# Hybrid decoder block on one core: banks copied whole by ScalarE before VectorE subtracts, gate sums started from zeros and bias, two late loads given a place

## The chip, the cores and the metric

The kernel runs on one core of one Trainium2 chip. The metric is the device time of one execution in microseconds (us), as the median of the runs; lower is better. Engines are named as in the profile: PE (TensorE, matmuls; PEld its weight loads), DVE (VectorE), ACT (ScalarE), POOL (GpSimd) and SP (SyncE, which here only issues loads). Each runs its own queue in order.

## The reference

One layer over 256 tokens of width 2048, in float32. All weights are read once, some 190 MB in all. Cut to what matters:

```python
ada = c @ w_ada + b_ada                          # 2048 -> 3 x 2048
shift, scale, gate = jnp.split(ada, 3, axis=-1)
h = rms_norm(x, g_pre) * (1.0 + scale) + shift
proj = h @ w_in                                  # q, k, v of two mixers, their gates, ma, mb
oa = nsa_attention(...)                          # compressed, selected and sliding-window keys
ya = (oa * silu(za)) @ w_br_a
ob = dilated_mixture(...)                        # three dilated windows
yb = (ob * silu(zb)) @ w_br_b
merged = sigmoid(ma) * ya + sigmoid(mb) * yb
out = merged @ w_out
return x + gate * rms_norm(out, g_post)
```

## The kernel before

Every large product is made from high and low parts. A float32 value is rounded to a PE format (fp32r) as its high part H, and the rest of it is the low part L; a product is H·H + H·L + L·H, three matmuls into one PSUM bank. Wherever a value becomes an operand there is thus a pair of steps: ACT copies it with rounding (H), DVE subtracts that copy from the source (L).

**Weights.** SP loads them in 512 KB pieces into seven buffers `raw`; `prep` (line 479) has ACT make `wH` (line 488) and DVE `wL` (line 489), three buffers of each; `product` (from line 536) issues the matmuls, which write banks of tag `mm` (four of the eight PSUM banks). The list `items` sets the order of the weights; between two items a step of the generator `side_main` (line 701) puts in a piece of everything else. A scheduler then sets the order of each engine's queue by its own estimate of when things are ready, so an edit moves neighbours too. It lets ACT and DVE read one PSUM tile only one after the other, in program order. `behind(i)` (line 212) makes an instruction follow instruction `i` on its own engine.

**Turns.** A tile that has to be transposed goes through PE into the bank of tag `pt`, of which there is one; the next user of that bank waits until the last reader is done. `turn_q` (line 822) turns two blocks of 128 queries: the bank's halves of 64 partitions (b = 0, 1) are copied by ACT into their own half of `AR` (line 832, H), and DVE writes the rest into the other half (line 833, L). `turn_k` (line 835) does the same for keys with two copies and two subtracts for each half (lines 844 to 847). `transA` (line 918) turns the probabilities P through a bank `pt_ps` (copy PH at line 925, subtract PL at 926); the scores `sA` (line 885) need AR. In the compressed branch the keys KC are copied by ACT and DVE (lines 747 and 748).

**The m stage.** When a quarter of 512 columns of the merged branches (MA) is complete, it is turned in two banks `m_ps` (one for 128 tokens each, line 1113; eight banks in all) into the operand of the last product. The target is split by the contraction tiles into groups of unequal length, since the high part lies in buffers freed by the low parts of h. For each group ACT makes mH (line 1119) and DVE mL (line 1120) in turn.

**The gate** is the last third of `ada`, summed on DVE: for each of 32 items of kind "gate" a 128x1024 piece of w_ada times one value of c per partition is added to `gacc` (two halves of 1024 columns, 16 items each). The first item of a half writes gacc with a TENSOR_SCALAR (line 507), the others add with SCALAR_TENSOR_TENSOR (line 509). A matmul with ones sums the partitions later; before it POOL adds the bias `bg` to row 0 (line 1140). The loads `gp` (g_post on all partitions, 1 MB), `bg` and `xr` (x again, 2 MB) are issued by ACT's queue (lines 1130 to 1135), as soon as the scheduler finds their buffers free.

## Time and profile before

| | us |
|---|---|
| median of 3 runs (lowest, highest) | 822.84 (822.63, 825.23) |
| the profiled execution | 823.05 |
| its span, first to last instruction | 821.3 |
| PE busy in it | 793.1 |
| DVE busy | 687.9 |
| ACT busy | 417.7 |
| POOL busy | 92.4 |

The span is what the trace shows; 1.75 us of the profiled execution lie outside it. PE is busy in 97% of the span at a granted clock of the upper level (2.4 GHz), so the places where PE pauses count, and the table of stretches, the list of waits and the timeline show where these are. A row of the timeline gives start and duration of an operation and, in brackets, how long its engine had been idle before it and what released it. The names are the program's: `m_ps` is a PSUM tile, `mL<-m_ps,mH` writes mL from the two others.

### The profile page before, as it was taken

The numbers are of one execution on the slowest core, as the hardware profiler recorded it, in microseconds if no ns is written. First come the engines' busy times: TensorE is split into PE (matmuls) and PEld (weight loads), VectorE is DVE, ScalarE is ACT, GpSimd is POOL, SyncE is SP. The second block draws the span as 40 slices with busy tenths as digits, with TensorE's granted clock in tenths as the row PEclk, the third lists the DMA queues.
The fourth block names the chain that finished last, engine by engine and source line by source line (L and its number), as shares of the span: only waits on it lengthen the run. The fifth ranks groups of instructions, "written<-read, shape, count | busy, mean of one in ns | idle before, by whom it ended". The sixth has DMA issues, their size and how long they took to land.

```text
span 821.3 us, 11929 instructions
## 1 busy us (share of the span) xinstructions
PE 793.1 (97%) x4160; PEld 667.3 (81%) x4160; DVE 687.9 (84%) x1068; ACT 417.7 (51%) x684; POOL 92.4 (11%) x111
## 2 busy tenths in 40 slices
PE   5999999999999999999999999999999999999995
PEld 4487888889887888888789999888887878888884
DVE  4799999999998879899888998867577999967455
ACT  2764263433434646566667666555644344445441
POOL 4200000000000026045412111001000010100000
PEclk9999999999999999999999999999999999999998
DMA  9899899999798547744444435655479999976533
GB/s 328 264 362 313 262 327 309 348 301 339 256 332 310 180 154 255 239 147 136 133 133 138 119 114 177 183 153 154 128 255 325 367 300 343 335 269 231 188 100 103
DMA packets 106950, 193.26 MB, mean 235 GB/s; under 512 B 7593, under 2 KB 36617, under 8 KB 106249
## 3 DMA queue, kind: packets, MB, share of 16 engines
q1 hardware_dynamic: 105376, 189.17, 69.5%
q10 hardware_dynamic: 1514, 3.33, 1.1%
q8 instruction: 33, 0.54, 0.3%
q14 instruction: 27, 0.22, 0.1%
HBM read 190.38 MB, written 2.10 MB: 234 GB/s over the span
## 4 chain that ended last, share of the span: by engine, by line
PE 85%; DVE 9%; issue 2%; DMA 2%; ACT 1%; DVEq 0%; ACTq 0%; SPq 0%
PE mm L558 21%; PE mm L561 21%; PE mm L559 21%; DVE wL L489 3%; PE mm L553 3%; PE mm L550 3%; PE mm L548 3%; PE mm L540 2%; DVE ST L509 2%; PE pt_ps L921 1%; PE sA L885 1%; PE ada_ps L183 1%; DMA xs<-in_x_dram 1%; DMA raw<-in_w_in_dram 1%; PE pvb_ps L1056 1%
## 5 line engine op out<-in xcount | busy, mean ns | idle before, releaser
L488 ACT ACTIVATE wH<-raw 128x1024 fp32r<-128x1024 f32 (+2 forms) x268 | 267.3, 1000 | 293.0 <-PE mm L559 182.3
L489 DVE TENSOR_TENSOR wL<-raw,wH 128x1024 fp32r<-128x1024 f32 (+2 forms) x268 | 316.4, 1185 | 74.1 <-ACT wH L488 69.2
L558 PE MATMUL mm<-wH,xH 128*128 128x512 f32 (+2 forms) x616 | 237.1, 387 | 1.3 <-DVE KB L631 1.1
L559 PE MATMUL mm<-wH,xL 128*128 128x512 f32 (+2 forms) x616 | 234.3, 382 | 0.0
L561 PE MATMUL mm<-wL,xH 128*128 128x512 f32 (+2 forms) x616 | 188.4, 383 | 0.4 <-DVE wL L489 0.4
L558 PEld LDWEIGHTS mm<-wH,xH 128*128 128x128 f32 x616 | 115.8, 188 | 23.0 <-issue 2.7
L559 PEld LDWEIGHTS mm<-wH,xL 128*128 128x128 f32 x616 | 115.9, 188 | 20.4 <-DVE xL L245 0.3
L561 PEld LDWEIGHTS mm<-wL,xH 128*128 128x128 f32 x616 | 113.1, 188 | 23.2 <-DVE wL L489 1.9
L509 DVE SCALAR_TENSOR_TENSOR ST<-raw,vecT,ST 128x768 f32<-128x768 f32 (+2 forms) x75 | 76.0, 1013 | 3.3 <-DMA raw<-in_w_ada_dram 3.1
L548 PE MATMUL mm<-xH,wH 128*128 128x256 f32 x240 | 63.5, 284 | 1.0 <-DVE VB L631 1.0
L550 PE MATMUL mm<-xL,wH 128*128 128x256 f32 x240 | 63.1, 283 | 0.0
L553 PE MATMUL mm<-xH,wL 128*128 128x256 f32 x240 | 50.0, 284 | 0.4 <-DVE wL L489 0.4
L558 PE MATMUL mm<-wH,yH 128*128 128x512 f32 x128 | 50.2, 392 | 0.0
L559 PE MATMUL mm<-wH,yL 128*128 128x512 f32 x128 | 50.0, 390 | 0.0
L558 PE MATMUL mm<-wH,mH 128*128 128x512 f32 x128 | 49.9, 390 | 0.0
L559 PE MATMUL mm<-wH,mL 128*128 128x512 f32 x128 | 49.9, 390 | 0.0
L548 PEld LDWEIGHTS mm<-xH,wH 128*128 128x128 f32 x240 | 45.9, 191 | 1.6 <-issue 1.6
L509 DVE SCALAR_TENSOR_TENSOR gacc<-raw,vecT,gacc 128x1024 f32<-128x1024 f32 x30 | 38.4, 1278 | 9.3 <-DMA raw<-in_w_ada_dram 9.3
L550 PEld LDWEIGHTS mm<-xL,wH 128*128 128x128 f32 x240 | 45.9, 191 | 0.0
L561 PE MATMUL mm<-wL,mH 128*128 128x512 f32 x128 | 39.8, 389 | 0.0
L561 PE MATMUL mm<-wL,yH 128*128 128x512 f32 x128 | 39.5, 390 | 0.0
L553 PEld LDWEIGHTS mm<-xH,wL 128*128 128x128 f32 x240 | 37.9, 192 | 0.8 <-DVE wL L489 0.8
(296 smaller groups left out, 1003.8 us busy)
## 6 DMA issues: line engine op xcount, KB each, us to landing
raw<-in_w_in_dram SPq DMA_DIRECT2D x165, 512.0 KB, 4.4
raw<-in_w_ada_dram SPq DMA_DIRECT2D x48, 512.0 KB, 5.5
raw<-in_w_ada_dram SPq DMA_DIRECT2D x48, 384.0 KB, 4.7
raw<-in_w_out_dram SPq DMA_DIRECT2D x32, 512.0 KB, 4.8
raw<-in_w_br_a_dram SPq DMA_DIRECT2D x16, 512.0 KB, 5.7
raw<-in_w_br_b_dram SPq DMA_DIRECT2D x16, 512.0 KB, 6.1
raw<-in_w_in_dram SPq DMA_DIRECT2D x29, 256.0 KB, 3.1
raw<-in_w_ada_dram SPq DMA_DIRECT2D x24, 256.0 KB, 4.9
```

Source lines behind the costliest of these rows:

```text
L183: T.matmul(ada0[:, half, j, :], lhsT=raws0[q][:, kk, half, j * 128:(j + 1) * 128], rhs=cT[:, kt:kt + 1].to_broadcast([128, 128]), start=(k ...
L488: A.activation(H, raw, AF.Copy)
L489: V.tensor_tensor(L, raw, H.bitcast(F32), op=OP.subtract)
L509: V.scalar_tensor_tensor(acc, r, cc, acc, op0=OP.mult, op1=OP.add)
L540: T.matmul(job.ps[t][:, :job.n], lhsT=hj[:, t * 128:(t + 1) * 128], rhs=it.raw[:, j, cs], start=(first and j == 0), stop=(last and j == it ...
L548: T.matmul(ps, lhsT=it.H[:, j, bs], rhs=sH[:, it.kt0 + j, :], start=(first and j == 0 and b == 0), stop=False, skip_group_check=True)
L550: T.matmul(ps, lhsT=it.H[:, j, bs], rhs=sL[:, it.kt0 + j, :], start=False, stop=False, skip_group_check=True)
L553: T.matmul(ps, lhsT=it.L[:, j, bs], rhs=sH[:, it.kt0 + j, :], start=False, stop=(last and j == it.nk - 1), skip_group_check=True)
L558: T.matmul(ps, lhsT=sH[:, it.kt0 + j, ts], rhs=it.H[:, j, cs], start=(first and j == 0), stop=False)
L559: T.matmul(ps, lhsT=sL[:, it.kt0 + j, ts], rhs=it.H[:, j, cs], start=False, stop=False)
L561: T.matmul(ps, lhsT=sH[:, it.kt0 + j, ts], rhs=it.L[:, j, cs], start=False, stop=(last and j == it.nk - 1))
L885: T.matmul(o, lhsT=QT[:, u.t, h // 2, h % 2, :], rhs=KTt[:, hl, :, 0:128] if u.t == 0 else KTt[:, hl, u.br, :], start=(hl == 0), stop=(hl ...
```

## The change

1. In the KC loop, in `turn_q`, in `turn_k` and in the m stage all ACT copies of a bank are issued first, and then all DVE subtracts. In the m stage one ACT copy of 128x512 writes a whole mH, and the low part is now what is split into groups.
2. `gacc` is made while attention still runs: POOL zeroes 128x1024 for each half, ACT's queue loads the bias (4 KB) into row 0, and all 32 items add with SCALAR_TENSOR_TENSOR. POOL's adds and the tile `bg` are gone.
3. The load of gp follows the last copy of the second block of the m stage, the reload of x the last copy of the fourth.

```diff
             acc = accs[it.piece][:, :, :it.n // 2]
         else:
-            if it.half not in gacc:
-                need("A")
-                gacc[it.half] = big.tile([128, 1024], F32, name=f"gacc{it.half}", tag=("cv", "k2")[it.half])
+            need("gacc")
             acc = gacc[it.half]
...
-                if it.kt0 + j == 0:
+                if it.kt0 + j == 0 and it.kind == "ada":
                     V.tensor_scalar(acc, r, cc, None, op0=OP.mult)
...
                     src = ps[64 * b:64 * (b + 1), a].rearrange("p t s -> p (t s)")
                     A.activation(KC[0:64, b, :], src, AF.Copy)
+                for b in range(2):
+                    src = ps[64 * b:64 * (b + 1), a].rearrange("p t s -> p (t s)")
                     V.tensor_copy(KC[64:128, b, 0:255], src[:, 1:])
...
                 A.activation(QT[own, t, :, b, :], ps[own], AF.Copy)
+            for b in range(2):
+                own, other = slice(64 * b, 64 * (b + 1)), slice(64 * (1 - b), 64 * (2 - b))
                 V.tensor_tensor(QT[other, t, :, b, :], ps[own], QT[own, t, :, b, :].bitcast(F32), op=OP.subtract)
...
                 A.activation(KTt[own, 0, b, :], psf[own], AF.Copy)
                 A.activation(KTt[other, 0, b, :], psf[own], AF.Copy)
+            for b in range(2):
+                own, other = slice(64 * b, 64 * (b + 1)), slice(64 * (1 - b), 64 * (2 - b))
                 V.tensor_tensor(KTt[own, 1, b, :], psf[own], KTt[own, 0, b, :].bitcast(F32), op=OP.subtract)
                 V.tensor_tensor(KTt[other, 1, b, :], psf[own], KTt[own, 0, b, :].bitcast(F32), op=OP.subtract)
...
+        for half in range(2):
+            gacc[half] = big.tile([128, 1024], F32, name=f"gacc{half}", tag=("cv", "k2")[half])
+            G.memset(gacc[half], 0.0)
+            A.dma_start(gacc[half][0:1, :], b_ada[0:1, 2 * D + half * 1024:2 * D + (half + 1) * 1024])
+        done.add("gacc")
...
-        mH, mL = Parts(), big.tile([128, KT, S], F32R, name="mL", tag="xH")
+        mH, mL = big.tile([128, KT, S], F32R, name="mH", tag="xH"), Parts()
         for a, b in groups:
-            mH.put(lows(a, b, "mH", F32R), a, b)
+            mL.put(lows(a, b, "mL", F32R), a, b)
+        turned = []
...
                 ts = slice(t * 128, (t + 1) * 128)
+                dH = mH[:, 4 * p:4 * p + 4, ts]
+                last = A.activation(dH, ps, AF.Copy, scale=0.5)
                 for a, b in groups:
                     a, b = max(a, 4 * p), min(b, 4 * p + 4)
                     if a < b:
-                        dH, o = mH.at[a]
-                        A.activation(dH[:, a - o:b - o, ts], ps[:, a - 4 * p:b - 4 * p], AF.Copy, scale=0.5)
-                        V.scalar_tensor_tensor(mL[:, a:b, ts], ps[:, a - 4 * p:b - 4 * p], 0.5,
-                                               dH[:, a - o:b - o, ts].bitcast(F32), op0=OP.mult, op1=OP.subtract)
+                        dL, o = mL.at[a]
+                        V.scalar_tensor_tensor(dL[:, a - o:b - o, ts], ps[:, a - 4 * p:b - 4 * p], 0.5,
+                                               dH[:, a - 4 * p:b - 4 * p].bitcast(F32), op0=OP.mult, op1=OP.subtract)
                 if t == NT - 1:
                     done.add(("mT", p))
+                    turned.append(last)
...
-        A.dma_start(gp, bass.AP(tensor=g_post.tensor, offset=g_post.offset, ap=[[0, 128], [1, D]]))
-        bg = big.tile([1, D], F32, name="bg", tag="qb")
-        A.dma_start(bg, b_ada[0:1, 2 * D:3 * D])
-        for t in range(NT):
-            A.dma_start(fin["x"][:, t, :], x[0, t * 128:(t + 1) * 128, :])
+        with behind(turned[1]):
+            A.dma_start(gp, bass.AP(tensor=g_post.tensor, offset=g_post.offset, ap=[[0, 128], [1, D]]))
+        with behind(turned[3]):
+            for t in range(NT):
+                A.dma_start(fin["x"][:, t, :], x[0, t * 128:(t + 1) * 128, :])
...
-            G.tensor_tensor(ga[0:1, :], ga[0:1, :], bg[:, half * 1024:(half + 1) * 1024], op=OP.add)
```

The lists below are pieces of the engines' queues. A row is line, operation, target and sources, shape, and the engines or load queues that it waits for; line numbers after the change are those of the new file.

In the m stage, DVE's queue at the first bank of the first quarter, before:

```order
L489 TENSOR_TENSOR wL<-raw,wH 128x1024 [waits DMAHW7_49,PE_49,Activation_49]
L1120 SCALAR_TENSOR_TENSOR mL<-m_ps,mH_6644 128x128 [waits Activation_49]
L509 SCALAR_TENSOR_TENSOR gacc_6339<-raw,vecT,gacc_6339 128x1024 [waits DMAHW0_49,DVE_49]
L1120 SCALAR_TENSOR_TENSOR mL<-m_ps,mH_6645 128x2x128 [waits Activation_49]
L507 TENSOR_SCALAR gacc_6780<-raw,vecT 128x1024 [waits DMAHW3_49]
L1120 SCALAR_TENSOR_TENSOR mL<-m_ps,mH_6646 128x128 [waits Activation_49]
L642 SCALAR_TENSOR_TENSOR MA<-MA,mm 128x512 [waits PE_49]
L489 TENSOR_TENSOR wL<-raw,wH 128x1024 [waits DMAHW1_49]
L1120 SCALAR_TENSOR_TENSOR mL<-m_ps,mH_6644 128x128 [waits Activation_49]
```

and after the change (the three groups' low parts are three tiles, so their numbers differ):

```order
L489 TENSOR_TENSOR wL<-raw,wH 128x1024 [waits DMAHW7_49,PE_49,Activation_49]
L1132 SCALAR_TENSOR_TENSOR mL_6649<-m_ps,mH 128x128 [waits Activation_49]
L1132 SCALAR_TENSOR_TENSOR mL_6650<-m_ps,mH 128x2x128
L1132 SCALAR_TENSOR_TENSOR mL_6651<-m_ps,mH 128x128
L507 SCALAR_TENSOR_TENSOR gacc_5632<-raw,vecT,gacc_5632 128x1024 [waits DMAHW3_49]
L489 TENSOR_TENSOR wL<-raw,wH 128x1024 [waits DMAHW1_49,PE_49,Activation_49]
L1132 SCALAR_TENSOR_TENSOR mL_6649<-m_ps,mH 128x128 [waits Activation_49]
L1132 SCALAR_TENSOR_TENSOR mL_6650<-m_ps,mH 128x2x128
L1132 SCALAR_TENSOR_TENSOR mL_6651<-m_ps,mH 128x128
```

The gacc rows that stood between the subtracts of one bank now stand behind them, and the TENSOR_SCALAR is a SCALAR_TENSOR_TENSOR.

PE's queue ahead of the second bank of that quarter, before; ahead of these rows stand the first bank and the twelve matmuls of one weight item:

```order
L558 MATMUL mm<-wH,yH_6244 128x512 [waits Activation_49]
L559 MATMUL mm<-wH,yL_6245 128x512
L558 MATMUL mm<-wH,yH_6244 128x512
L559 MATMUL mm<-wH,yL_6245 128x512
L561 MATMUL mm<-wL,yH_6244 128x512 [waits DVE_49]
L561 MATMUL mm<-wL,yH_6244 128x512
L558 MATMUL mm<-wH,yH_6244 128x512
L559 MATMUL mm<-wH,yL_6245 128x512
L1113 MATMUL m_ps<-ident,MA 128x128 [waits DVE_49,PE_49]
L1113 MATMUL m_ps<-ident,MA 128x128 x3
```

and after the change, where the first bank and six matmuls of the same item stand ahead of these rows:

```order
L556 MATMUL mm<-wH,yH_6250 128x512
L557 MATMUL mm<-wH,yL_6251 128x512
L556 MATMUL mm<-wH,yH_6250 128x512
L557 MATMUL mm<-wH,yL_6251 128x512
L559 MATMUL mm<-wL,yH_6250 128x512 x2
L1124 MATMUL m_ps<-ident,MA 128x128 [waits DVE_49,Activation_49]
L1124 MATMUL m_ps<-ident,MA 128x128 x3
L556 MATMUL mm<-wH,yH_6250 128x512
L557 MATMUL mm<-wH,yL_6251 128x512
```

The second bank's transposes moved up by one weight item: twelve matmuls of 128x512 stand between the two banks, where there were twenty.

In attention, ACT's queue at the third `turn_k` (the one at 410 us in the trace of before), before:

```order
L488 ACTIVATE wH<-raw 128x1024 [waits DMAHW1_49,PE_49,Activation_49]
L844 ACTIVATE AR<-k_ps 64x256 [waits PE_49]
L845 ACTIVATE AR<-k_ps 64x256
L488 ACTIVATE wH<-raw 128x1024 [waits DMAHW2_49,PE_49,Activation_49]
L844 ACTIVATE AR<-k_ps 64x256 [waits DVE_49]
L845 ACTIVATE AR<-k_ps 64x256
L488 ACTIVATE wH<-raw 128x1024 [waits DMAHW3_49,PE_49,Activation_49]
```

and after the change:

```order
L488 ACTIVATE wH<-raw 128x1024 [waits DMAHW1_49,PE_49,Activation_49]
L846 ACTIVATE AR<-k_ps 64x256 [waits PE_49]
L847 ACTIVATE AR<-k_ps 64x256
L846 ACTIVATE AR<-k_ps 64x256
L847 ACTIVATE AR<-k_ps 64x256
L488 ACTIVATE wH<-raw 128x1024 [waits DMAHW2_49,PE_49,Activation_49]
```

The four copies of one bank stand together, and the weight copy that stood between them follows.

PE's queue behind the same turn, ahead of the next user of the bank, before (ahead of these rows stand twelve matmuls of 128x512, four sA and three of the four ot_ps rows):

```order
L558 MATMUL mm<-wH,xH 128x512
L559 MATMUL mm<-wH,xL_2455 128x512
L561 MATMUL mm<-wL,xH 128x512
L558 MATMUL mm<-wH,xH 128x512
L559 MATMUL mm<-wH,xL_2455 128x512
L561 MATMUL mm<-wL,xH 128x512
L558 MATMUL mm<-wH,xH 128x512 [waits Activation_49]
L559 MATMUL mm<-wH,xL_1570 128x512
L558 MATMUL mm<-wH,xH 128x512
L559 MATMUL mm<-wH,xL_1570 128x512
L921 MATMUL pt_ps<-ident,P 128x128 [waits DVE_49,PE_49,Pool_49]
L921 MATMUL pt_ps<-ident,P 128x128 x3
```

and after the change (ahead of these rows the same twelve matmuls):

```order
L889 MATMUL sA<-AR 128x256 [waits Activation_49]
L889 MATMUL sA<-AR 128x256 x3
L947 MATMUL ot_ps<-PH,VR 128x256 [waits DVE_49,PE_49,Activation_49]
L925 MATMUL pt_ps<-ident,P 128x128 [waits DVE_49,PE_49,Pool_49]
L925 MATMUL pt_ps<-ident,P 128x128 x3
L949 MATMUL ot_ps<-PL,VR 64x256
L947 MATMUL ot_ps<-PH,VR 128x256
L949 MATMUL ot_ps<-PL,VR 64x256
```

The transposes into pt_ps moved up past three rows of ot_ps and ten matmuls of 128x512.

## Rows read from the trace of the kernel before

**Rows 1.** Busy time of each engine, share of the span, instructions (the page's first part).

```profile
PE 793.1 (97%) x4160; PEld 667.3 (81%) x4160; DVE 687.9 (84%) x1068; ACT 417.7 (51%) x684; POOL 92.4 (11%) x111
```

**Rows 2.** Stretches: limits, length, busy time of PE, PEld, DVE, ACT, POOL, clock, DMA.

```profile
350.00:500.00 150.00, 147.86 (x981) 132.38 (x981) 136.43 (x266) 101.73 (x259) 44.90 (x56) 1.00 0.44 130
600.00:650.00 50.00, 49.61 (x220) 40.75 (x218) 40.71 (x40) 22.01 (x24) 0.00 (x0) 1.00 0.89 319
650.00:700.00 50.00, 48.39 (x221) 39.71 (x220) 49.13 (x56) 20.91 (x27) 2.37 (x1) 1.00 0.95 332
```

**Rows 3.** PE's waits from 300 to 740 us: for whom; total, times, longest (us).

```profile
PE m_ps L1113 <- DVE mL L1120: 1.6, 1, 1.6
PE pt_ps L921 <- DVE AR L833: 0.7, 2, 0.5
PE pt_ps L921 <- DVE AR L847: 0.7, 1, 0.7
PE q_ps L829 <- DVE PL L926: 0.6, 2, 0.3
```

**Rows 4.** Timeline of the m stage's first quarter: start, duration, engine, line, operation.

```profile
657.03 0.60 PE L1113 MATMUL m_ps<-ident,MA 128*128 128x128 f32 x4
...
657.74 0.26 ACT L1119 ACTIVATE mH<-m_ps 128x128 fp32r<-128x128 f32 x1
657.86 1.23 DVE L489 TENSOR_TENSOR wL<-raw,wH 128x1024 fp32r<-128x1024 f32 x1
...
659.21 1.27 DVE L509 SCALAR_TENSOR_TENSOR gacc<-raw,vecT,gacc 128x1024 f32<-128x1024 f32 x1
...
660.40 0.41 DVE L1120 SCALAR_TENSOR_TENSOR mL<-m_ps,mH 128x256 fp32r<-128x256 f32 x1
...
660.56 2.37 POOL L1140 TENSOR_TENSOR gacc<-gacc,bg 1x1024 f32<-1x1024 f32 x1 [79.65 <-DVE gacc L509]
...
660.73 2.75 DVE L507 TENSOR_SCALAR gacc<-raw,vecT 128x1024 f32<-128x1024 f32 x1
...
661.60 0.39 PE L558 MATMUL mm<-wH,yH 128*128 128x512 f32 x1
...
661.83 0.39 PE L559 MATMUL mm<-wH,yL 128*128 128x512 f32 x1
663.40 0.28 DVE L1120 SCALAR_TENSOR_TENSOR mL<-m_ps,mH 128x128 fp32r<-128x128 f32 x1
...
663.83 0.63 PE L1113 MATMUL m_ps<-ident,MA 128*128 128x128 f32 x4 [1.61 <-DVE mL L1120]
```

**Rows 5.** Timeline around the load of gp, from DVE, ACT's queue and PE.

```profile
602.37 0.75 DVE L507 TENSOR_SCALAR gacc<-raw,vecT 128x1024 f32<-128x1024 f32 x1
...
606.28 0.36 ACTq L1130 DMA_DIRECT2D gp<-in_g_post_dram  x1
...
614.52 1.28 DVE L509 SCALAR_TENSOR_TENSOR gacc<-raw,vecT,gacc 128x1024 f32<-128x1024 f32 x1 [4.52 <-DMA raw<-in_w_ada_dram]
...
617.00 0.50 PE L561 MATMUL mm<-wL,xH 128*128 128x512 f32 x1 [0.39 <-DVE wL L489]
```

**Rows 6.** Groups from 340 to 500 us: total and mean (ns); idle before.

```profile
L925 ACT ACTIVATE PH<-pt_ps 128x512 fp32r<-128x512 f32 x23 | 13.7, 597 | 7.6 <-PE pt_ps L921 7.2
```

**Rows 7.** The group of POOL's largest memsets.

```profile
L750 POOL MEMSET BL<- 128x32 f32 x4 | 0.6, 156 | 254.2 <-DVE BL L754 242.6 <-DVE mf L301 11.7
```

**Rows 8.** Timeline of the third key turn.

```profile
410.48 0.38 PE L840 MATMUL k_ps<-ident,K 128*128 128x128 f32 x2
...
411.45 0.37 ACT L844 ACTIVATE AR<-k_ps 64x256 fp32r<-64x256 f32 x1
411.59 1.77 DVE L489 TENSOR_TENSOR wL<-raw,wH 128x1024 fp32r<-128x1024 f32 x1 [0.52 <-ACT wH L488]
...
416.88 0.52 PE L921 MATMUL pt_ps<-ident,P 128*128 128x128 f32 x3
```

**Rows 9.** DVE's longest wait from 676 to 720 us: total, times, longest (us).

```profile
DVE wL L489 <- ACT wH L488: 0.8, 1, 0.8
```

## The prediction

> **What bounds the kernel now.** I read the busy shares first [rows 1]: TensorE (PE) is busy 793.1 of 821.3 us, so what a change can win is the time in which PE stands still. The next view is the table of stretches [rows 2]: from 350 to 500 us PE is busy 147.86 of 150 us, from 600 to 650 us 49.61 of 50, from 650 to 700 us 48.39 of 50. These are the three stretches in which most of the edited code runs, and they lack 2.1, 0.4 and 1.6 us. VectorE (DVE) is busy 49.13 of 50 us in the last one: there a wait of PE is a place in DVE's queue, not a long operation. Third, the list of PE's waits says whom it waits for [rows 3]: once for 1.6 us for the m stage's low part, 0.7 + 0.7 + 0.6 us for the bank tagged pt behind attention's turns and PL. That list counts a little less than starts show: before the next m_ps the last matmul starts at 661.83, one follows another by 0.23 us (661.60 to 661.83), so the next could start at 662.06, and starts at 663.83 [rows 4]: 1.77 us. Measured so, the pauses of over 0.15 us between 340 and 490 us number ten, from 0.16 to 0.84 us, and make 3.9 us. The edited steps thus have some 1.8 + 0.4 + 3.9 = 6.1 us to give.
>
> **The m stage: -1.8 us.** One m_ps bank is copied and subtracted in three groups, in turn by ACT and DVE, because the two engines' reads of one bank stand one after the other. Each of DVE's three subtracts is queued behind something longer [rows 4]: behind wL (657.86, 1.23 us), behind a gacc (659.21), and the last behind the second gate half's first TENSOR_SCALAR, which takes 2.75 us (660.73) while a POOL add of 2.37 us runs (660.56); the same form takes 0.75 us at 602.37 with POOL idle [rows 5]. So the last subtract starts at 663.40, 5.8 us after the transposes' end (657.03 + 0.60). Changed: one ACT copy of 128x512, for which PH, the same shape from the same kind of bank, gives 0.60 us [rows 6]; then three subtracts side by side, 0.28 + 0.41 + 0.28 = 0.97 us [rows 4]. By the order they stand behind the same wL, which ends at 657.86 + 1.23 = 659.09, when the copy (657.74 + 0.60 = 658.34) is done: the last ends at 660.06, and with 0.15 us for the hand-over (663.40 + 0.28 to 663.83) the bank is free at 660.2. PE gets to the second m_ps earlier, since the scheduler counts on the shorter chain: only 12 matmuls stand between, 12 x 0.23 = 2.8 us from 657.6, so 660.4. It arrives as the bank has just come free, and the pause of 1.77 us goes. What is late next: nothing in the list, since the other three blocks have no listed wait now and shed the same exchanges. Bounds: all of it (-1.8), or, if one item like wL (1.23 us) still comes between, -0.6. I take -1.8, as the order shows none.
>
> **Gate sums.** SCALAR_TENSOR_TENSOR takes the place of TENSOR_SCALAR: 1.27 us [rows 4] for 2.75 once (POOL's add is gone from there) and for 0.75 once [rows 5]: on DVE a gain of 1.0 us. It ends on no path of its own; DVE feeds PE through wL. The two zeroings of 128x1024 on POOL have no like in this trace: the nearest is a memset of 128x32, 156 ns [rows 7]; 32 times that is 5 us, all of it a fixed cost 0.2. One comes at about 451 us, right behind a P product and in the middle of a k turn, the other near 500 us. What POOL does to DVE's wL is seen at 411.59: 1.77 us beside a P product, against 1.23 [rows 4, 8]. Twice 0.54 us is my upper bound, 0 the lower (PE has a stock of weights): I take +0.1, near the lower, since PE is full in most stretches where P products run. The Trainium skill (GPSIMD Engine Reference, Key points) says that POOL shares its SBUF interfaces with VectorE, and contends with two-port modes and with two-input operations; the stretched wL, which reads two SBUF tensors, agrees. ACT's two bias DMAs of 4 KB wait for a memset, and behind the first stand PH and the next wH. By the order it comes after the k turn's copies, and PH is not due before the bank changes hands: nothing.
>
> **gp tied back: -0.4 us.** Issued at 606.28 it takes 1 MB out of a stream that is busy at 0.89 [rows 2, 5]. DVE then waits 4.52 us for a gate row (at 614.52), the wL queued behind that is late, and PE waits 0.39 us for it before 617.00. That goes. The new place, behind the second block's last copy, lies in the stretch where the transfers are busier still, 0.95 [rows 2]. 1 MB at its 332 GB/s is 3.2 us more for the stream. But DVE's longest listed wait between 676 and 720 us is 0.8 us, for ACT, and none is for a load [rows 9], so there is a stock, and PE holds two further weights: 0 to 0.4 us may come back, and I take 0. The x reload keeps its place: its buffer is that of MA, free only after the last transposes.
>
> **Attention's turns: -0.2 us, the widest term.** The serial work is the same (k: four copies of 0.37, four subtracts of 0.42), but the copies now stand together, and no wL or wH gets between. Take the k turn at 410.48 [rows 8]. Before: copies from 411.45, the first subtract behind a wL that ends at 411.59 + 1.77 = 413.36, the second pair late behind more of the kind, pt_ps at 416.88. Changed: the copies end at 411.45 + 4 x 0.37 = 412.9, the subtracts run from 413.36 to 415.05, pt is free at 415.2: 1.7 us earlier. But the scheduler pulled the next pt_ps up as well: by the order PE has 12 matmuls of 128x512 and 5 of half the columns behind the transposes (end 410.86), 12 x 0.23 + 5 x 0.12 = 3.3 us, and is there at 414.1: a pause of 1.1 us where there was 0.2. I walked the ten pauses in this way, with the copies' and subtracts' own first starts and the order's matmuls between: this one loses 0.9, the first k turn, whose scores now come six matmuls behind it, 0.4, a new one of 0.3 comes up ahead of that; two keep 0.6 each (0.84 and 0.70 before), three small ones go (0.7), and the two for PL go (1.0), as more matmuls stand ahead of them. Sum 3.7 against 3.9. Bounds: with no queue ahead of a chain they all vanish (-3.9); with one weight operation (1.23 us, rows 4) more ahead of each of the four k chains, +4.9.
>
> **KC's loops** (near 300 us): the same copies in another order, in a stage where PE waits for weights; 0, at most 0.3 either way.
>
> **Sum.** -1.8 - 0.4 - 0.2 + 0.1 = -2.3 on the profiled execution's 823.05, which is 820.75. The median of the runs lies 0.2 below the profiled one: **820.5 us**.
>
> **Rivals.** (1) *Turns really get short*: if no weight operation stands ahead, the chains come to 2.2 (q) and 3.8 us (k), which the matmuls behind nearly all turns cover, and half to all of 3.9 us goes: 820.5 - 1.8 = 818.7, at best 816.8. For it: the listed pauses there all end with a turn or PL. Against: at 411.45 the copy came 1 us after the transposes' start, and the subtracts behind a wL. (2) *Tight turns, slower*: the scheduler placed the next pt_ps by its own idea of the chain, 3.3 to 4.1 us behind a k turn, where my walk makes the chain 3.9 to 4.8 us. One weight operation of 1.23 us more ahead of each of four k turns: 820.5 + 4.9 = 825.4; with the memsets' 1.1 826.5. From +2.3 us on the gain is gone. For it: the walk's 1.1 us at 414. Against: the other three k turns came out at 0.8 or less. (3) *The pauses only move*: gp's 0.4 comes back in the busier stretch, and 1.2 us of the m pause stays behind another DVE item where DVE is 98% busy [rows 2]: 820.5 + 1.6 = 822.1. For it: these shares. Against: the order has the subtracts side by side. The Trainium skill (DMA: Bandwidth & Descriptors, Issuing engines are not separate DMA queues) says that DMAs of all queues interleave on the same 16 engines; by that rule gp's load is moved and not made cheaper, and its term would be 0.
>
> **How the numbers follow.** 0.3%, about what a measurement here tells from no change, is 2.5 us: 820.4 to 825.3 is no change. My forecast lies at that edge: chance 0.44, half on either side. Rival 1: 0.16, faster. Rival 2: 0.20, of it 0.12 slower and 0.08 within. Rival 3: 0.20, within. So faster 0.22 + 0.16 = 0.38, same 0.22 + 0.08 + 0.20 = 0.50, slower 0.12. The range reaches beyond half of rival 1 (818.3) and to rival 2 with three of its four k turns late (820.5 + 3.7 = 824.2, taken as 824.3).
>
> **What the profile after would show.** m stage: no wait of PE for mL over 0.3 us, and the three subtracts within 1.1 us. Near 615 us: no wait of DVE for a gate row of 4 us; near 690 us such a wait if rival 3 holds. Turns: copies and subtracts in blocks; PE's waits for pt_ps, q_ps and sA near 2 us in all as now; under 0.7 means rival 1, over 4 rival 2. The memsets: 0.2 to 5 us each, with the wL beside them under 1.8 us. The forecast would be wrong if PE is short of weights (waits for wL) between 440 and 510 us, or if the whole mH makes matmuls wait for copies.

## The result

The changed kernel is slower: 828.69 us median of six runs (827.26 to 829.61) against 823.24 (822.63 to 826.45) for the kernel before, a ratio of 1.0057 (95% interval 1.0038 to 1.0075). The forecast was 820.5 with 824.3 as its upper end. The profiled execution of the changed kernel took 829.08 us, its span 827.3, 6.0 us above the span before.

The busy line of the page (compare [rows 1]: PE 793.1 of 821.3) shows 1.3 us more of busy time on PE, for the same 4160 matmuls, and so 4.7 us more of standing still:

```profile
PE 794.4 (96%) x4160; PEld 668.8 (81%) x4160; DVE 685.0 (83%) x1068; ACT 416.1 (50%) x674; POOL 87.4 (11%) x111
```

The table of stretches says where (limits, length, busy time of PE, PEld, DVE, ACT, POOL, granted clock, DMA share, GB/s). After the change:

```profile
300.00:350.00 50.00, 48.21 (x301) 41.98 (x300) 41.45 (x77) 29.06 (x50) 15.52 (x18) 1.00 0.68 216
350.00:500.00 150.00, 145.89 (x971) 131.81 (x970) 133.74 (x259) 99.68 (x249) 43.93 (x57) 1.00 0.44 132
600.00:650.00 50.00, 50.00 (x220) 40.94 (x219) 40.34 (x40) 22.37 (x24) 0.00 (x0) 1.00 0.86 289
650.00:700.00 50.00, 47.06 (x207) 38.08 (x207) 45.37 (x52) 18.64 (x20) 0.00 (x0) 0.97 0.92 327
700.00:750.00 50.00, 48.36 (x222) 39.77 (x221) 37.37 (x43) 20.35 (x22) 0.00 (x0) 1.00 0.89 308
```

The two stretches of before that [rows 2] do not hold:

```profile
300.00:350.00 50.00, 48.49 (x303) 42.51 (x302) 40.49 (x72) 28.37 (x43) 16.09 (x20) 1.00 0.71 225
700.00:750.00 50.00, 50.00 (x228) 40.70 (x227) 39.60 (x45) 23.11 (x30) 3.30 (x1) 1.00 0.82 286
```

PE's busy time falls by 0.28, 1.97, -0.39, 1.33 and 1.64 us from one to the other: 4.8 us in all, which with the 1.3 us of longer matmuls is the 6 us. DVE, which was busy 49.13 of 50 us from 650 to 700 us [rows 2], is busy 45.37: it now waits there itself.

PE's longest waits from 300 to 740 us name two causes (for whom; total, times, longest):

```profile
PE m_ps L1124 <- DVE mL L1132: 4.4, 2, 2.8
PE pt_ps L925 <- DVE AR L835: 2.4, 5, 0.6
PE pt_ps L925 <- DVE AR L851: 1.7, 3, 0.7
```

In [rows 3] these were 1.6, 0.7 and 0.7; the waits for PL are gone. The timeline of the m stage's first quarter (start, duration, engine, line, operation; in brackets idle time ahead and its releaser) stands beside [rows 4]:

```profile
658.01 0.66 PE L1124 MATMUL m_ps<-ident,MA 128*128 128x128 f32 x4
...
658.47 1.22 DVE L489 TENSOR_TENSOR wL<-raw,wH 128x1024 fp32r<-128x1024 f32 x1
...
658.70 0.60 ACT L1127 ACTIVATE mH<-m_ps 128x512 fp32r<-128x512 f32 x1
...
659.60 0.68 DVE L643 TENSOR_TENSOR MA<-MA,MB 128x512 f32<-128x512 f32 x1
...
660.21 1.22 DVE L489 TENSOR_TENSOR wL<-raw,wH 128x1024 fp32r<-128x1024 f32 x1
...
661.34 1.28 DVE L507 SCALAR_TENSOR_TENSOR gacc<-raw,vecT,gacc 128x1024 f32<-128x1024 f32 x1
...
662.54 1.22 DVE L489 TENSOR_TENSOR wL<-raw,wH 128x1024 fp32r<-128x1024 f32 x1
...
663.67 0.81 DVE L1132 SCALAR_TENSOR_TENSOR mL<-m_ps,mH 128x128 fp32r<-128x128 f32 x3
...
664.63 1.04 PE L1124 MATMUL m_ps<-ident,MA 128*128 128x128 f32 x4 [2.80 <-DVE mL L1132]
```

The copy takes the 0.60 us that were predicted and the three subtracts 0.81 us together (0.97 predicted), and the bank is copied by 659.30. But DVE comes to the subtracts only at 663.67: one sum, one MA step and three wL stand ahead, work that DVE had not yet done when the transposes ran. PE has nothing left to do from about 661.7 and stands still (2.96 us by starts, against 1.77 before). From the transposes' start to the last subtract's end the bank is held for 6.5 us (658.01 to 664.48), with twelve matmuls to cover it. The same returns at the third quarter: the transposes start at 708.54, the subtracts at 712.65, and PE's next ones at 713.55 with 1.64 us of wait, where before there was no pause at all.

### The profile page after: what moved, and what is told of

Read it like the earlier page. It is cut to its first block, busy times and chain, and to the rows that moved or that the text cites. A ratio compares the mean times of both kernels' runs of the same rounds, so it can differ in the third digit from the quotient of the medians.

```text
span 827.3 us, 11916 instructions
## 1 busy us (share of the span) xinstructions
PE 794.4 (96%) x4160; PEld 668.8 (81%) x4160; DVE 685.0 (83%) x1068; ACT 416.1 (50%) x674; POOL 87.4 (11%) x111
## 4 chain that ended last, share of the span: by engine, by line
PE 80%; DVE 11%; issue 3%; DMA 2%; ACT 2%; DVEq 0%; ACTq 0%; SPq 0%
PE mm L557 20%; PE mm L556 20%; PE mm L559 20%; DVE wL L489 3%; PE mm L551 3%; PE mm L546 3%; PE mm L548 3%; PE mm L538 2%; DVE ST L507 2%; DMA raw<-in_w_ada_dram 2%; PE pt_ps L925 2%; PE sA L889 1%; ACT wH L488 1%; PE ada_ps L183 1%; DMA xs<-in_x_dram 1%
## 5 line engine op out<-in xcount | busy, mean ns | idle before, releaser
L507 DVE SCALAR_TENSOR_TENSOR gacc<-raw,vecT,gacc 128x1024 f32<-128x1024 f32 x32 | 41.0, 1280 | 13.4 <-DMA raw<-in_w_ada_dram 13.2
```

Of the source, the lines that this page charges most:

```text
L507: V.scalar_tensor_tensor(acc, r, cc, acc, op0=OP.mult, op1=OP.add)
```

## Experiments

**Theory, formed from the two traces.** DVE works its queue strictly in order. A gate sum can run only when its own load has landed; if it stands ahead of a wL whose load was issued earlier, it holds up finished weights, and DVE falls behind. The lag is paid where PE next needs DVE at once: at m_ps. By DVE's queues, 28 of the 32 gate sums of the changed kernel stand ahead of such wLs, 22 of the kernel before. The run-up to the first m bank, from DVE's queue (w a wL, m an mL, G a gate sum, its number how many wLs of earlier loads stand behind it):

```
before  G2 w w G2 w G2 w G2 w G2 w G2 w G2 w w w G w m G m G2 m
after   G3 w w G3 w G3 w G3 w w G2 w G2 w G2 w G2 w w G1 w m m m G2
```

**Rivals:** the m stage's own edit (whole copy, the second transposes moved up); gp's load in its new place; more DVE time in the gate sums. For attention: the turns' order, in `turn_q` or in `turn_k`.

The diffs below are cut to the lines that tell most; `...` stands for lines left out. Each ratio is to the kernel before, measured beside that run.

### One part at a time: the late pauses

Gate sums alone (item 2 of the change):

```diff
-                gacc[it.half] = big.tile([128, 1024], F32, name=f"gacc{it.half}", tag=("cv", "k2")[it.half])
+            need("gacc")
...
```

> The kernel before with the gate part alone changed (zeros by POOL, bias by ACT's queue, all sums as SCALAR_TENSOR_TENSOR, POOL's adds gone). Theory A: DVE's queue now takes gate sums further ahead of weights whose loads were issued earlier, so DVE waits for loads (9 to 13 us as in the changed kernel) and comes late to m_ps: one or two m pauses, together 2.5 to 4 us against 1.8, time +1 to +2 us (824.5). Rival B (memsets disturb the turns): attention's pauses rise by 1 us or more. Rival C (the m edit loses): m pauses as before or shorter, since the 2.75 us operation beside POOL's add is gone; time -0.5 to -1.5 us (822).

1.0030 (1.0013 to 1.0047), 825.93 us. PE waits 2.7 us for mL in the first quarter, with the old exchange of three copies and three subtracts and with gp in its old place, so neither is needed for the long pause. Attention is as before (157.70 us busy from 340 to 500, 157.67 before): the memsets and bias DMAs cost nothing there.

The two late loads alone (item 3):

```diff
+        with behind(turned[1]):
+            A.dma_start(gp, bass.AP(tensor=g_post.tensor, offset=g_post.offset, ap=[[0, 128], [1, D]]))
...
```

> The kernel before with the two late loads alone tied behind the m stage's copies. Theory A (gate sums' place in DVE's queue): here too the sums moved up against the weights; the pause at 616 us (0.5) goes, the m pauses grow to 2.5 us or more; time +0.5 to +1.5 us. Rival C: the pause at 616 us goes and nothing else changes, time -0.5 us; or, if gp collides with the stream at about 690 us, DVE waits there for gate rows for 2 to 4 us and PE pauses by up to 1 us, time +0.5.

0.9987 (0.9970 to 1.0004), 822.59 us. The pause near 616 us goes and the m pause grows to 3.21 us, both as expected: the scheduler gave the gate sums other places here too (25 of 32 ahead). What one end wins the other loses; the longer time that was expected does not show.

The changed kernel without item 3:

```diff
-        with behind(turned[1]):
-            A.dma_start(gp, bass.AP(tensor=g_post.tensor, offset=g_post.offset, ap=[[0, 128], [1, D]]))
...
+        A.dma_start(gp, bass.AP(tensor=g_post.tensor, offset=g_post.offset, ap=[[0, 128], [1, D]]))
...
```

> The changed kernel with the two load ties undone (gp again as soon as its buffer is free, at about 606 us). Theory A with the second pause put down to gp's new place (DVE waits 2.65 us for gate rows at 697 to 701 us, just behind gp's issue at 689, and the pause of 1.8 us follows at 711): that pause goes, the one at 661 stays at 2 to 3 us, a pause of 0.5 to 1.5 may come back at 616; time -0.5 to -2 us against the changed kernel, 827.5. Rival (the second pause is the shorter cover of 12 matmuls): pauses at 661 and 711 stay, time as the changed kernel or +1.

1.0023 (1.0006 to 1.0041), 826.45 us, against 1.0057 of the changed kernel; the two intervals still touch. gp is issued at 609.4 again; the first quarter's pause stays at 2.96 us and the third quarter's is gone. So the tie makes the second pause and not the first. The pause near 616 us, which might have come back, did not: PE is busy for all 50 us from 600 to 650. In the changed kernel gp is issued at 689.23, and DVE then stands idle 0.71 us at 697.76 and 1.94 us at 700.98 for gate rows, 8 to 11 us ahead of the third quarter's transposes. The Trainium skill (DMA: Bandwidth & Descriptors, Issuing engines are not separate DMA queues) says that the transfers of all queues interleave on the same 16 engines. The trace agrees so far: behind the moved load DVE waits 2.65 us for gate rows. Whether the transfer alone makes the second pause is not separated, since undoing the tie moved the sums too (25 of 32 ahead of earlier loads' wL, 28 in the changed kernel).

The m stage alone (item 1, m stage only):

```diff
+                last = A.activation(dH, ps, AF.Copy, scale=0.5)
...
```

> The kernel before with the m stage alone changed (one whole ACT copy, then the subtracts). Theory A (the late loss comes from where gate sums stand in DVE's queue, which the gate and load edits moved): the first m pause of 1.8 us goes, no other comes, time -1.5 to -2 us (821.5). Rival C (the m edit itself loses: only 12 matmuls stand between two banks, and DVE cannot do three subtracts in that time behind its other work): pauses of 2.5 to 3 and about 1.8 us in the m stage as in the changed kernel, time +2 to +3 us (826).

0.9966 (0.9948 to 0.9984), 821.31 us: shorter by a little, beyond the interval. PE's wait for mL falls to 0.3 us (0.51 by starts). Near 616 us PE waits 1.3 us for wL. The first rival falls: the edit itself does not lose. Its gain has two parts that this run does not separate, the shorter exchange and the slow TENSOR_SCALAR of [rows 4], which here comes behind the subtracts (at 666.18) and takes 0.74 us. And 21 of 32 sums still stand ahead of earlier loads' wL, so such an order can make the long pause and need not.

### The order of the gate sums

`lastw` holds the last wL issued; each gate sum is put behind it. Nothing else is changed by hand: no load is given a place, no operation is added; the scheduler still orders the rest anew.

```diff
+            lastw[:] = [V.tensor_tensor(L, raw, H.bitcast(F32), op=OP.subtract)]
...
-        with behind(*(first_h if i < 8 else ())):
+        with behind(*(first_h if i < 8 else lastw if it.kind == "gate" else ())):
```

On top of the changed kernel:

> The changed kernel with one thing added: each gate sum on DVE is held behind the low weight (wL) whose load was issued just before its own, so that DVE takes them in the order of the loads. In the changed kernel 28 of 32 sums stand ahead of earlier loads' wL, in the kernel before 22, nearer together. Theory A (sums ahead of the weights make DVE wait for loads with finished weights behind it, which comes due at m_ps): DVE's wait for gate loads falls from 13 to under 6 us, wL is done 2.3 to 4 us after wH starts instead of 5 to 7, the m pauses of 3.0 and 1.8 us shrink to under 0.6 each; attention as in the changed kernel; time -3 to -5 us against it, 824. Rival D (DVE simply has too much work from 640 to 715 us, in whatever order): the same sum of pauses, 828.5.

0.9972 (0.9959 to 0.9986), 821.78 us, 0.85% or 7 us below the changed kernel and more than the pauses alone had let expect: in the profiled executions PE stands still 4.9 us less, which is the two pauses, and is busy 3.9 us less (790.5 for 794.4), of which the clock at the end of this document explains a part. PE is never idle in the late stretches:

```profile
650.00:700.00 50.00, 50.00 (x230) 41.37 (x229) 48.60 (x57) 20.53 (x22) 0.00 (x0) 1.00 0.99 366
700.00:750.00 50.00, 50.00 (x229) 40.84 (x228) 40.09 (x47) 23.81 (x28) 0.00 (x0) 1.00 0.83 292
```

The first m bank (timeline of this kernel):

```profile
655.98 0.60 PE L1125 MATMUL m_ps<-ident,MA 128*128 128x128 f32 x4
...
658.05 0.81 DVE L1133 SCALAR_TENSOR_TENSOR mL<-m_ps,mH 128x128 fp32r<-128x128 f32 x3
...
659.19 0.60 PE L1125 MATMUL m_ps<-ident,MA 128*128 128x128 f32 x4
```

The bank is held for 2.9 us (655.98 to 658.86) where it was 6.5, with the same twelve matmuls to cover it. The sums, their durations, the zeroings, the whole copies and gp's late place (issued at 681.7) are all still there, and the rival of longer sums falls with that; so does gp's late place as a cause of its own. With the order, no sum stands ahead of a wL of an earlier load. Attention keeps its loss (155.72 us busy from 340 to 500).

On top of the kernel before, alone:

> The kernel before with one thing alone: each gate sum on DVE held behind the low weight whose load was issued just before its own. Theory A: no wait of DVE for a gate load and no pause at 616 us; the m pause stays, at 1 to 2 us, since the three subtracts of a bank still stand behind wL and gate sums; time -1 to -2.5 us, 821.5. Rival E (the order of the loads is the whole late effect and the m edit gives nothing): as e6 with both, 818.7.

0.9944 (0.9924 to 0.9965), 819.84 us: one dependency and nothing else beats the kernel before. Theory A had expected the m pause to stay at 1 to 2 us. It went, with the old exchange in three groups all there: PE has no listed wait from 596 to 740 us. The first bank's last subtract, PE's next transposes, and the row that stood ahead of that subtract in [rows 4]:

```profile
659.29 0.28 DVE L1121 SCALAR_TENSOR_TENSOR mL<-m_ps,mH 128x128 fp32r<-128x128 f32 x1
...
659.83 0.60 PE L1114 MATMUL m_ps<-ident,MA 128*128 128x128 f32 x4
...
665.33 0.73 DVE L508 TENSOR_SCALAR gacc<-raw,vecT 128x1024 f32<-128x1024 f32 x1
```

The bank is held for 5.2 us (from 654.36) where it was 6.65 (657.03 to 663.68). The order moved the second half's first sum behind the subtracts, away from POOL's add, and it takes 0.73 us instead of 2.75. So in the kernel before that one row made much of the pause, as the prediction read it; the changed kernel has neither that row nor the add, and its longer pause is DVE's arrears.

How arrears come about is seen one weight at a time. ACT rounds a weight (wH), DVE then makes its wL. With the order (timeline of this kernel):

```profile
635.06 1.06 ACT L489 ACTIVATE wH<-raw 128x1024 fp32r<-128x1024 f32 x1 [1.66 <-PE mm L560]
...
636.15 1.23 DVE L490 TENSOR_TENSOR wL<-raw,wH 128x1024 fp32r<-128x1024 f32 x1 [1.49 <-ACT wH L489]
```

In the changed kernel (timeline of ACT and DVE at the like place):

```profile
635.68 1.06 ACT L488 ACTIVATE wH<-raw 128x1024 fp32r<-128x1024 f32 x1 [1.77 <-PE mm L557]
...
636.87 1.28 DVE L507 SCALAR_TENSOR_TENSOR gacc<-raw,vecT,gacc 128x1024 f32<-128x1024 f32 x1 [1.81 <-DMA raw<-in_w_ada_dram]
638.07 1.22 DVE L489 TENSOR_TENSOR wL<-raw,wH 128x1024 fp32r<-128x1024 f32 x1
639.35 1.28 DVE L507 SCALAR_TENSOR_TENSOR gacc<-raw,vecT,gacc 128x1024 f32<-128x1024 f32 x1
640.55 1.22 DVE L489 TENSOR_TENSOR wL<-raw,wH 128x1024 fp32r<-128x1024 f32 x1
```

The wL of the weight rounded at 635.68 is the one at 640.55. DVE stood idle 1.81 us for a gate row while a finished weight was queued behind it. From wH's start to wL's end it is 2.32 us with the order, and 640.55 + 1.22 - 635.68 = 6.09 us here. Over the last three weights that ACT rounded ahead of the first m bank's transposes this lag was 3.6, 2.6 and 2.3 us in the kernel before, 7.4, 6.4 and 6.0 in the changed one, 6.8, 5.8 and 5.6 with the gate sums alone, 5.3, 4.9 and 4.7 with the loads alone, and 3.7, 3.9 and 3.8 with the order alone. DVE's waits for gate rows from 596 to 720 us in these: 9.3, 13.2, 9.2 and 8.8 us, and none in the ordered kernels. Neither figure ranks the kernels by itself. The sum of the waits hardly does. The lag tells the changed kernel and the gate sums alone from the ordered ones, but the order alone has more of it than the kernel before and no pause, and the loads alone (lag 4.7 to 5.3) had the longest pause, because their slow TENSOR_SCALAR (2.54 us beside a POOL add, as in [rows 4]) comes on top. What the order does to the m pauses is thus shown by the runs with and without it; that the lag is its only way is not.

With the m stage's edit as well:

> The kernel before with the m stage changed and gate sums held in the order of the loads. Theory A: the pause at 615 us that m alone kept (1.4 us in its profile, beside the load of gp) shrinks to under 0.5, no m pause over 0.5 us, time -1 us against m alone, 820. Rival D: as m alone, 821.3.

0.9931 (0.9904 to 0.9957), 818.66 us, no late pause. Its interval overlaps that of the order alone, so what the whole copy still adds can't be told.

### gp out of the late stretch

gp is loaded in three tiles while attention ends, into buffers that are free by then, and the second gate half goes where gp was; with the m stage's edit, unordered:

```diff
+        gp = [big.tile([128, n], F32, name=f"gp{o}", tag=tag) for o, n, tag in ((0, 1024, "k2"), (1024, 512, "vs"), (1536, 512, "vw"))]
...
+                gacc[it.half] = big.tile([128, 1024], F32, name=f"gacc{it.half}", tag=("cv", "zb")[it.half])
```

> As e7 (m stage changed, gp loaded early), but with the gate sums left where the scheduler puts them: 25 of 32 ahead of earlier loads' wL, as in the kernel with the loads tied. Theory A: it is the order that counts and not gp's place: DVE waits 8 to 12 us for gate loads, wL comes due late at m_ps, one pause of 2.5 to 3.5 us near 660; time 821 to 822.5, 3 to 4 us above e7. Rival F (gp's load was what kept DVE waiting): no pause above 0.5 us, time as e7, 817.6.

0.9948 (0.9927 to 0.9968), 819.71 us. The pause near 616 us is gone, those at the m banks are 0.74 and 1.22 us: 1.6 us of listed wait for mL is still there, and DVE waits 8.1 us for gate rows. Both expectations missed: the pauses are under theory A's 2.5 to 3.5 us and over rival F's 0.5. From 600 to 700 us PE lacks 1.64 us here and 1.63 with the m stage alone, so in the profiles the earlier load moved the loss and did not lessen it, and the two intervals overlap. With the order:

> As the m stage changed and sums in the order of loads, and gp loaded in three parts into buffers that attention leaves (k2, vs, vw), between 490 and 600 us, where the transfers are busy for half the time; the second half of the gate's sum lies in zb instead of k2. Theory A: no load of 1 MB in the full stretches, so DVE waits under 3 us for gate loads from 600 to 715 us and PE has no pause over 0.3 us there: 600 to 715 us complete, time 819.5 to 820. Rival D: a pause of 1 us or more stays in the m stage, 821.

0.9920 (0.9894 to 0.9946), 817.64 us, the shortest time here; no late pause. It beats both kernels, though not the order alone, nor the order with the m stage, by more than the intervals.

### Attention's turns

`turn_q` and `turn_k` alone, no other part:

```diff
                 A.activation(QT[own, t, :, b, :], ps[own], AF.Copy)
+            for b in range(2):
+                own, other = slice(64 * b, 64 * (b + 1)), slice(64 * (1 - b), 64 * (2 - b))
                 V.tensor_tensor(QT[other, t, :, b, :], ps[own], QT[own, t, :, b, :].bitcast(F32), op=OP.subtract)
```

> The kernel before with turn_q and turn_k alone changed (copies first, then subtracts). Theory A (the parts add up, and attention's loss is the turns' own: the next bank user was pulled up by more than the chains got shorter): PE's waits for pt_ps behind turns rise from 1.4 to about 4 us, the pauses between 340 and 490 us from 3.9 to about 6, time +2 us (825), the m stage as in the kernel before (one pause of 1.8 us). Rival B (POOL's memsets and ACT's bias loads disturb the turns): attention's pauses stay near 4 us, time within 0.5 us of before. Rival C (everything late is the m edit): says nothing else here.

1.0013 (0.9996 to 1.0030), 825.41 us. The time alone can't tell, PE's busy time can: 155.89 us of 340 to 500, where the kernel before has 157.67 and those with the m stage, the gate sums, the loads, the order, or m stage and order edited have 157.68 to 157.84. The loss of attention is the turns' own.

Each of them by itself (the same hunk, in one function):

```diff
                 A.activation(KTt[other, 0, b, :], psf[own], AF.Copy)
+            for b in range(2):
...
```

> The kernel before with turn_q alone changed. Theory A (a turn loses where its next pt user was pulled up by more than the chain got shorter): by the order the matmuls behind the q turns fall from 5.9, 3.2, 3.7, 3.6, 4.7 to 4.1, 3.1, 3.1, 2.5, 3.5 us; pauses behind q turns rise from 1.3 to about 3 us, k turns stay as in the kernel before; pauses from 340 to 490 us about 5, time +1 us at most. Rival: the loss sits in the k turns alone (four copies before the first subtract): 3.9 us of pauses, no change.

> The kernel before with turn_k alone changed. Theory A: the matmuls behind the k turns fall from 5.8, 6.0, 6.0, 4.7 to 3.7, 3.9, 3.3, 3.6 us; pauses behind k turns rise from 1.4 to about 2.5 us; some q turns are closer too; pauses from 340 to 490 us about 5, time +1 us at most. Rival: the loss sits in the q turns: 3.9 us of pauses or less, no change or a gain.

`turn_q` alone: 1.0010 (0.9987 to 1.0034), 824.76 us, PE busy 156.34 of 160; `turn_k` alone: 0.9998 (0.9978 to 1.0017), 824.09 us, 156.85. Losses of 1.3 and 0.8 us in the profiles, 1.8 together, so both rivals fall, each function loses, and more than half is from the query turns. Not tried, since the kernel has no means for it: the new order of the turns with PE's old spacing.

## Why the prediction was wrong

**The sum.** Predicted -2.3 us on the span, measured +6.0:

| term | predicted | measured |
|---|---|---|
| m stage | -1.8 | +1.33 (650 to 700 us) and +1.64 (700 to 750), and some 1.3 of slower matmuls |
| gate sums | +0.1 | 0 in attention; their new places are part of the m row |
| gp | -0.4 | -0.39 near 616 us, not by the tie alone; the pause at 711 us in the m row |
| turns | -0.2 | +1.97 (350 to 500 us) and +0.28 (300 to 350 us) |
| KC | 0, at most 0.3 | nothing seen: the turns alone lose 0.31 us from 300 to 350 us with the KC loop as before |

**m stage: the failed step is "By the order they stand behind the same wL, which ends at 657.86 + 1.23 = 659.09".** The order of the instructions was right, and the copy and the subtracts cost what was said. Wrong was DVE's clock time at that point: it was taken from the trace of before, where DVE had hardly any arrears. The wL directly ahead of the subtracts ended not at 659.1 but at 662.54 + 1.22 = 663.76. The text costed the sums' duration ("on DVE a gain of 1.0 us") and not their place. "What is late next: nothing" failed for the same reason at the third quarter. What was said of PE was near: 2.8 us of matmuls behind the transposes, and it had 3.0 (658.7 to 661.7).

**Gate sums.** The zeroings took 0.95 us each, far under the 5 us that [rows 7] were scaled to, and cost PE nothing:

```profile
452.60 0.95 POOL L1029 MEMSET gacc<- 128x1024 f32 x1
```

What the edit does cost, gate alone +0.30%, is the sums' order, which no term held.

**gp.** The first half was right to 0.01 us, but by luck. The pause near 616 us was 0.55 us by starts in the kernel before and 1.45 to 2.36 in the four kernels that left gp there and kept the old sums (m stage, turns, q and k alone), three of them (the turns) with all gate sums in the very order of the kernel before. And the gate sums alone and the changed kernel without the tie load gp in the old place (608.5 and 609.4) and have no pause there. So the tie alone removes it, and the new sums' places alone do too. The second half ("so there is a stock", from [rows 9]) failed: in the changed kernel the gate rows that DVE needs there come late, and its queue stands. Rival 3 named this and gave 0.4 us; the third quarter lost 1.64.

**Turns: the failed step is "with the copies' and subtracts' own first starts".** Where the start of a chain was the same, the walk was right: the turn at 414 came out at 0.84 us (1.1 predicted), two kept 0.63 and 0.64 (0.6 each predicted), and the waits for PL went. But five pauses that the walk let go stayed or grew (0.75, 0.80, 0.70, 0.34 and 0.67 us, between 355 and 401 us). The pauses over 0.15 us make 6.0 us, against 3.9 before and 3.7 predicted. (By the changes that the walk lists, its sum is 3.9 + 0.9 + 0.4 + 0.3 - 0.3 - 0.7 - 1.0 = 3.5 and its term -0.4; that 0.2 us is no part of the miss.) One of the five, the query turn at 359 us, after the change:

```profile
358.96 0.38 PE L829 MATMUL q_ps<-ident,QA 128*128 128x128 f32 x2
...
359.15 1.05 ACT L488 ACTIVATE wH<-raw 128x1024 fp32r<-128x1024 f32 x1
...
359.82 1.04 POOL L920 TENSOR_TENSOR P<-P,cf 128x512 f32<-128x512 f32 x1 [1.91 <-DVE cf L918]
...
360.10 0.76 ACT L832 ACTIVATE AR<-q_ps 64x256 fp32r<-64x256 f32 x2
360.24 1.70 DVE L489 TENSOR_TENSOR wL<-raw,wH 128x1024 fp32r<-128x1024 f32 x1 [0.59 <-ACT wH L488]
...
361.97 0.86 DVE L835 TENSOR_TENSOR AR<-q_ps,AR 64x256 fp32r<-64x256 f32 x2
...
362.97 0.63 PE L925 MATMUL pt_ps<-ident,P 128*128 128x128 f32 x4 [0.64 <-DVE AR L835]
```

The copies stand together now, but behind a wH, and the subtracts behind that weight's wL, stretched from 1.22 to 1.70 us by a P product. In the kernel before, the copy at this turn started 0.5 us after the transposes and the next pt_ps did not wait. From the transposes' start to the last subtract's end it is 3.9 us (358.96 to 362.83) where it was 3.2, and pt_ps had been pulled up. That is rival 2's mechanism at less than half its price: 2.0 us of PE's time, where "One weight operation of 1.23 us more ahead of each of four k turns" gave 4.9. The rival was named for the key turns only; the query turns lost more.

**The rivals together.** Rival 2 (+4.9) and rival 3 (+1.6) were given 0.20 each, as if one excluded the other. Here parts of both came true at once, with something that neither held.

## To carry over

On an engine that works in order, an operation that waits for its own load should not stand ahead of one whose data have come: before costing an edit by durations, list each queue's rows with the loads that they wait for, since a scheduler that is handed an unrelated edit may swap them, and one dependency that puts the patient work behind the urgent was worth 0.6% here. A chain's start is not to be taken from the trace of before when the order changes: walk each engine's queue from the last point at which it stood idle. Where a chain is made short on paper, look whether its consumer was pulled up by as much.

## What the runs showed of the hardware

**The clock after a pause.** In the changed kernel PE stood still from 661.7 to 664.6 us, and the granted clock then fell to the lower of its two levels (1.2 and 2.4 GHz). Stretches after the change (columns as above):

```profile
662.00:664.00 2.00, 0.00 (x0) 0.00 (x0) 2.00 (x4) 0.48 (x1) 0.00 (x0) 1.00 0.87 266
664.00:666.00 2.00, 1.37 (x6) 1.30 (x7) 2.00 (x4) 0.30 (x1) 0.00 (x0) 0.68 0.84 290
666.00:668.00 2.00, 2.00 (x6) 1.54 (x5) 1.54 (x4) 0.30 (x1) 0.00 (x0) 0.50 1.01 390
668.00:670.00 2.00, 2.00 (x10) 1.63 (x9) 1.03 (x2) 0.81 (x1) 0.00 (x0) 0.97 0.95 337
```

PE's row counts six matmuls from 666 to 668 us and ten in the next 2 us: a price of the pause on top of the pause. The same fall followed the m pauses of 2.36, 2.86, 2.96 and 2.40 us (both turns, gate alone, without the tie of gp, k turns alone), and none followed those of 1.77, 1.80 and 1.96 us (kernel before, changed kernel's third quarter, q turns alone). With the loads alone PE stood still longer, 3.21 us, and the clock held:

```profile
662.00:664.00 2.00, 0.00 (x0) 0.00 (x0) 2.00 (x2) 1.06 (x1) 0.96 (x1) 1.00 0.91 354
664.00:666.00 2.00, 1.01 (x7) 0.95 (x8) 2.00 (x4) 0.28 (x1) 0.00 (x0) 1.00 1.05 404
```

One kernel goes either way from execution to execution. In the profiles here a mean granted clock of 0.995 or less over the whole execution goes with such a fall, and 0.996 or more with none. By that mark all six executions of the changed kernel had one, two of ten with the loads alone, none of the 28 of the four ordered kernels, and 35 of the 81 of the kernel before that were measured beside the experiments: their median is 825.6 us, that of the other 46 822.9. So part of what the order wins may be executions without a fall; what decides between the two is open. Open is also the 2 us or so by which PE's total busy time differs between ordered kernels (790.5 to 791.8) and the profiled execution of the kernel before (793.1), which had no such fall.

**A POOL operation on one partition.** In the kernel with the order alone, a wL that takes 1.22 us elsewhere takes 2.85 beside POOL's add of one row:

```profile
659.46 2.40 POOL L1141 TENSOR_TENSOR gacc<-gacc,bg 1x1024 f32<-1x1024 f32 x1 [80.54 <-DVE gacc L510]
...
660.09 2.85 DVE L490 TENSOR_TENSOR wL<-raw,wH 128x1024 fp32r<-128x1024 f32 x1
```

The Trainium skill (GPSIMD Engine Reference, Key points) says that POOL shares its SBUF interfaces with VectorE and contends with operations of two SBUF inputs. wL is one, and the trace agrees; the size, 1.6 us from a row of 4 KB, is the trace's. The change removed that add; no run shows what this alone is worth.
